# A two-block transformer on one core: feed-forwards that begin with the input matmuls, and conditioning products moved into the context stage

## The chip, the cores and the metric

The kernel runs on one core of one Trainium2 chip. The metric is the device time of one execution in microseconds (us), as the median of several runs. The core has five engines with instruction streams of their own: TensorE (PE: matmuls and, as matmuls with an identity, transposes), VectorE (DVE), ScalarE (ACT), GpSimd (POOL) and SyncE (SP), which here issues the transfers from device memory. Each engine takes its instructions strictly in the order in which the kernel put them.

## The reference, cut to what matters

One sequence of 256 tokens of width 1024 goes through two blocks. The first has two layers; each layer is, with `rmsnorm` around every step:

```
h = h + 0.5 * rmsnorm(swiglu(rmsnorm(h, g[0]), ffn1_w_in[i], ffn1_w_out[i]), g[1])
...  mix = even_mixer (layer 0) or odd_mixer (layer 1)
h = h + rmsnorm(mix, g[3])
h = h + 0.5 * rmsnorm(swiglu(rmsnorm(h, g[4]), ffn2_w_in[i], ffn2_w_out[i]), g[5])
...  a gated per-layer embedding
```

where `swiglu(x, w_in, w_out) = (silu(gate) * up) @ w_out` with a hidden width of 2816. The second block also has two layers, a pooling mixer and an attention, each followed by a squared-relu MLP of hidden width 4096. Its norms are modulated by a conditioning vector, for the main ("latent") tokens and, up to the attention, for 256 context tokens of their own:

```
s_lat, s_ctx = silu(c), silu(c_ctx)
sh1, sc1, g1, sh2, sc2, g2 = split(s_lat @ ada_w[i] + ada_b[i], 6)      # the same with s_ctx for the context
...
h_lat = h_lat + g2 * (square(relu(m_l @ mlp_w1[i])) @ mlp_w2[i])        # layer 0: for the context too
```

`s_lat @ ada_w[i]` needs nothing of the first block, so it can be worked out at any time before it is used.

## The kernel before

All arithmetic is fp32 in effect. A matrix product is three matmuls of split operands (high part by high, high by low, low by high; `mm3`, lines 251 to 254). Weights come as chunks of 128 x 1024 (512 KB) through SP's queue into a ring of four tiles, `rawm`; ScalarE rounds a chunk to its high part `whm` (line 244), VectorE subtracts to get the low part `wlm` in two halves (line 247). Seven such pairs are held; a pair's place comes free when the matmuls of the pair seven chunks earlier are done.

A feed-forward (`ffn`, line 472 on) works through pairs of hidden groups. The first group (`first`) is worked out token-major: matmuls `g` (line 252 to 254, by `group512`), Silu on ScalarE and product with the up part on VectorE (`sil`, line 482), four transposes on TensorE (`tpsm`, line 429), split into `hid`. `rb_of` (line 409) spreads the reciprocal norms over columns (`dg` on VectorE, `rbpm` on TensorE). All later groups (`inp`) are feature-major, without transposes: 48 matmuls `finm` fill a PSUM bank half with gate and half with up, twice per group; VectorE, ScalarE and VectorE again (`sil`, lines 496 to 498) finish it. The output matmuls `acc` follow some groups behind.

The conditioning products are no matmuls: the weights arrive transposed, and VectorE multiplies each 128 x 1024 half chunk (`rawa`) by the conditioning row and sums along it, in one instruction (`ada_chunk`, line 1013, written to a junk tile `jka`; the sum goes to `adacol`). There are 48 chunks of two halves; 32 of them serve latent and context and take two products per half. They are handed out to the feed-forwards and the odd mixer by the list `cuts`, as filling with low priority: a half chunk is loaded by SP between the weight loads. `ada_finish` adds the biases, makes the norm factors and turns the gates into rows in device memory (transposes `adtf`, line 1035).

`mlp0` is the MLP of layer 0 for both token sets. In its loop `both(i)` does 96 matmuls for hidden group i, 24 of the context (`cfinf`) and 24 latent (`mfinm`) by turns; `relu2` takes each PSUM bank through a tile `rl` (ScalarE relu, VectorE square, split into `hich` and `hicl`, or `hidh` and `hidl`); `out(i - 1)` does 24 matmuls `cfof`, which VectorE adds into `ac`, and 24 `acc`. Tiles come from pools; a tile with the same tag as others waits, in the order in which the program asks for them, until an earlier one of its `bufs` buffers is no longer read.

The order within each engine is settled ahead of the run by a scheduler from priorities and from such dependences.

Of the kernel before, what the change touches and what calls it, by code (L numbers as in the profile page):

```python
# [173 lines left out]
def tile_model(ctx: ExitStack, tc: tile.TileContext, A, out):  # L174
# [44 lines left out]
    M = Res()  # L219
# [31 lines left out]
    def mm3(o, a, b, first, last):  # L251
        T.matmul(o, a[0], b[0], start=first, stop=False)  # L252
        T.matmul(o, a[0], b[1], start=False, stop=False)  # L253
        T.matmul(o, a[1], b[0], start=False, stop=last)  # L254

    def hilo(hi, lo, src):
        ins = S.activation(hi, src, AF.Copy)  # L257
# [109 lines left out]
    def junction(acc, gb, mul, e, x, g, pre=None, act=None):  # L367
        def rstd(t):
            sm = ssq2(halves(acc[t]), 1.0 / (32 * mul))
            return ms_r(sm, e[t] if e is not None else epst[:, (0 if mul == 1.0 else 1):(1 if mul == 1.0 else 2)])[1:]  # L370

        def scaled(t, n):
            sl = slice(512 * n, 512 * n + 512)
            y = tp.tile([128, 512], F32, name="yt", tag="yt", bufs=3)
            V.tensor_tensor(y, acc[t][:, sl], gb[:, sl], op=ALU.mult)
            return y

        def add(t, n, y, r):
            sl = slice(512 * n, 512 * n + 512)
            return V.scalar_tensor_tensor(h[:, t, sl], y, r, h[:, t, sl], op0=ALU.mult, op1=ALU.add).ins  # L380

        done_ = [None]

        def step(t):
            with after(done_[0]):
                if pre is not None:
                    pre(t)
                r, _ = rstd(t)
                ys = [scaled(t, n) for n in range(2)]
                for n in range(2):  # L390
                    with after(done_[0]):
                        done_[0] = add(t, n, ys[n], r)
                    if x.xt is not None:
                        ins = feed(x, t, n, g)
            if x.xt is not None and t == 0:
                with tc.issue_after(ins):
                    if act is not None:
                        warm(act)
            if t == 1:
                if x.xt is None:  # L400
                    for t in range(2):
                        stats(x, t)
                elif x.stats:
                    with tc.issue_after(ins):
                        for t in range(2):
                            stats(x, t)
        return step

    def rb_of(x):
        ps = bank(name="rbp")  # L410
# [56 lines left out]
    def feat_tile(ps, w, xt):  # L467
        for k in range(8):
            a = (w[0][:, 128 * k:128 * k + 128], w[1][:, 128 * k:128 * k + 128])
            mm3(ps, a, (xt[0][:, k, :], xt[1][:, k, :]), k == 0, k == 7)  # L470

    def ffn(x, win, wout, np_, pool, hooks, joint, side=None):
        def first():
            hid = xt_tiles(2, pool, "hid", 4)
            ps = group512(win[0:2], x.xt, True)
            for t in range(2):
                if x.r[t] is None:
                    stats(x, t)
            for t in range(2):
                s = pool.tile([128, 256], F32, name="sil", tag="sil", bufs=2)  # L480
                S.activation(s, ps[:, t, 0:256], AF.Silu, scale=x.r[t])
                V.tensor_tensor(s, s, ps[:, t, 256:512], op=ALU.mult)
                t_split(s, 2, hid, t)
            return hid

        hids = [first()]
        rb = rb_of(x)

        def inp(i):
            hid = xt_tiles(2, pool, "hid", 4)  # L490
            for j in range(2):
                ps = bank(name="fin")
                for u in range(2):
                    feat_tile(ps[:, 256 * u:256 * u + 256], split(M, win[2 * i + j], u), x.xt)
                s = pool.tile([128, 256], F32, name="sil", tag="sil", bufs=2)
                V.tensor_tensor(s, ps[:, 0:256], rb, op=ALU.mult)
                S.activation(s, s, AF.Silu)
                V.tensor_tensor(s, s, ps[:, 256:512], op=ALU.mult)  # L498
                hilo(hid[0][:, j, :], hid[1][:, j, :], s)
            return hid  # L500

        acc = None
        for i in range(1, np_):
            hids.append(inp(i))
            if i == 1 and side is not None:
                with behind(seen[0]):
                    side()
            if i == HOLD:
# [123 lines left out]
    def even_block(l, x, nx, ng):  # L632
# [5 lines left out]
        with tc.tile_pool(name="ev", bufs=1, reuse_waits="tile") as ev:  # L638
# [218 lines left out]
            for b in range(2):  # L857
# [5 lines left out]
            out_kn(A["evo"][0], acc, yts[0], 0, True, False)  # L863
            out_kn(A["evo"][2], acc, ys, 0, False, False)
            out_multi([(A["evo"][3], ys, 2), (A["evo"][1], yts[1], 0)], acc, False, True,
                      junction(acc, gb, 1.0, None, x2, ng))
        return x2

    def odd_block(l, x, nx, ng):
# [138 lines left out]
    def ada_chunk(l, i, who, sv, r, jk):  # L1008
        for f in range(2):
            src = r.raw.tile([128, 1024], F32, name="rawa", tag="raw" + r.tag, bufs=2)  # L1010
            Y.dma_start(src, A["adw"][l, i][:, 1024 * f:1024 * f + 1024])
            for v in who:
                V.scalar_tensor_tensor(jk, src, 1.0, sv[v], op0=ALU.mult, op1=ALU.mult,  # L1013
                                       accum_out=adacol[:, l, v, 2 * i + f:2 * i + f + 1])

    def silu_vec(v, tile_):
# [1 line left out]
        S.activation(tile_, tile_, AF.Silu)  # L1018
        return tile_

    def ada_finish(l, v, r, pool):
# [4 lines left out]
        if n == 48:  # L1026
            V.scalar_tensor_tensor(gsc[:, l, v, 1], col[:, 32:40], 1.0, ng2[:, l, 1], op0=ALU.add, op1=ALU.mult)
            stage = pool.tile([128, 2, 8], F32, name="stage", tag="stage", bufs=1)
            if l == 0:
                V.tensor_tensor(stage[:, 0], col[:, 16:24], psc, op=ALU.mult)  # L1030
            else:
                V.tensor_copy(stage[:, 0], col[:, 16:24])
            V.tensor_copy(stage[:, 1], col[:, 40:48])
# [155 lines left out]
    def mlp0(rr, cx, pre):  # L1189
        with tc.tile_pool(name="lm0", bufs=1, reuse_waits="tile") as lm:  # L1190
            g = gload(rows[1])
            gc = cx.rp.tile([128, 1024], F32, name="prow", tag="prow", bufs=3)
            Y.dma_start(gc, rows[3].partition_broadcast(128))
            ac = cx.sp.tile([128, 2, 1024], F32, name="ac")
            xt = xt_tiles()
            al = alloc_in(lm)
# [61 lines left out]
            hids[1][0] = inp((bank(name="mfin"), xt, "hid", w1))  # L1258
            acc = acc_tiles()
            out_l(0, w2, acc, True)  # L1260
            for i in range(2, 16):
                hids.append(both(i))
                if i < 14:
                    out(i - 1, acc)
                if i == 4:
                    for v in range(2):
                        ada_finish(1, v, AD, lm)
            out(13, acc)
            js = (14, 15)
            ws = [split(M, A["m2"][0, j], i) for j in js for i in range(2)]  # L1270
            cxt = xt_tiles(8, cx.xp, "cxT")

            def rstd(t):
                for n in range(2):
# [259 lines left out]
        Y.dma_start(out[128:256, half(0)], hf[:, half(0)])  # L1534
        S.dma_start(out[128:256, half(1)], hf[:, half(1)])

    def side_ada(pool, chunks):
        who = (0, 1) if any(c[2] for c in chunks) else (0,)
        jk = pool.tile([128, 1024], BF16, name="jka1", tag="jka1")
        tiles = [pool.tile([128, 1024], F32, name="sv1", tag="sv1", bufs=2) for _ in who]  # L1540

        def run():
            p = tc.cur_priority
            tc.cur_priority = p + FILL // 2
            r = Res()
            r.raw, r.tag = pool, "s"
            sv = [silu_vec(v, tiles[v]) for v in who]
            for l, i, both in chunks:
                ada_chunk(l, i, (0, 1) if both else (0,), sv, r, jk)
            tc.cur_priority = p  # L1550

        return run
# [6 lines left out]
    AD = Res()  # L1559
    AD.bank, AD.tag = pfl, "f"  # L1560

    def fin0(pool):
        for v in range(2):
            ada_finish(0, v, AD, pool)

    x = new_x()
    for t in range(2):
# [1 line left out]
            feed(x, t, n, gcol[:, 0, 0])  # L1569

    lat = [(0, i, True) for i in range(24)] + [(1, i, i < 8) for i in range(24)]
    cuts = {(0, 1): lat[:9], (0, 2): lat[9:20], (1, 1): lat[20:30], (1, 2): lat[30:45], (1, 0): lat[45:]}

    def plain():
        return new_x(False)
# [6 lines left out]
    for l in range(2):  # L1582
        x = ffn_block(l, 1, x, new_x, gcol[:, l, 1], cuts[l, 1], None if l else {2: setup, 5: rope2})
        x = (odd_block if l else even_block)(l, x, new_x, gcol[:, l, 2])
        x = ffn_block(l, 2, x, plain, None, cuts[l, 2], {5: fin0} if l else None)
        if l == 1:
            cx = Res()
            cx.tag, cx.bank, cx.nsm = "f", pfl, 8
# [57 lines left out]
```

## Time and profile before

| what | value |
| --- | --- |
| runs | 1895.53, 1896.07, 1900.37 us; median 1896.07 |
| profiled execution | 1896.52 us |
| its span, first to last instruction | 1894.5 us |
| busy in the span: PE, DVE, ACT | 97%, 70%, 49% |
| mean granted TensorE clock | 0.992 of full speed |
| HBM read | 349.92 MB, 185 GB/s over the span |

Times in the views count from the start of the span. The idle time of an engine that is not the bottleneck costs nothing. The start of a matmul is exact, its end is modelled, so the pace of a row of matmuls is read from one start to the next.

### The profile page before, as it was taken

The page shows a single profiled execution, that of the slowest core. Times are in us where ns is not written, and L with a number is a line of the kernel's source. Part 1 is how long each engine was busy: PE and PEld are TensorE (multiplying, and loading weights), DVE is VectorE, ACT ScalarE, POOL GpSimd, SP SyncE. Part 2 cuts the span into 40 slices and gives each one's busy share as a digit, 9 for nine tenths or more (in the row PEclk, how much of TensorE's full clock was granted, in tenths as well). Part 3 has the DMA queues.
Part 4 walks back from the last instruction along what each step waited for, and adds up shares of the span by engine and source line. Part 5 has one row for each costly group of instructions (what it writes and reads, how often), then busy time and mean ns, then how long its engine had stood idle before and what let it go on. Part 6 is the DMA issues. An engine that isn't in the chain of part 4 may idle for free.

```text
span 1894.5 us, 29709 instructions
## 1 busy us (share of the span) xinstructions
PE 1834.9 (97%) x11425; PEld 1615.8 (85%) x11425; DVE 1332.2 (70%) x2522; ACT 927.3 (49%) x1463; POOL 57.8 (3%) x96
## 2 busy tenths in 40 slices
PE   7999999999999999999999999899999999999998
PEld 6999777899969998888789898789999987667997
DVE  6998666899679976856588877744444478556555
ACT  6645756644474445444454456533223235544443
POOL 0000000000000000000000000100000002000000
PEclk9999999999999999999999999999999999999999
DMA  7887534788568875755589865432333314226652
GB/s 265 286 284 244 172 101 144 259 274 273 177 215 277 272 241 192 247 172 161 168 282 307 298 195 201 135 110 90 108 96 98 98 60 147 78 68 187 197 191 81
DMA packets 100181, 352.93 MB, mean 186 GB/s; under 512 B 12296, under 2 KB 13128, under 8 KB 100040
## 3 DMA queue, kind: packets, MB, share of 16 engines
q1 hardware_dynamic: 99320, 350.17, 56.7%
q8 instruction: 89, 1.46, 0.3%
q10 hardware_dynamic: 720, 0.88, 0.1%
q14 instruction: 52, 0.43, 0.1%
HBM read 349.92 MB, written 1.08 MB: 185 GB/s over the span
## 4 chain that ended last, share of the span: by engine, by line
PE 85%; DVE 5%; ACT 4%; DMA 3%; issue 2%; POOL 1%; SPq 0%; POOLq 0%; ACTq 0%; DVEq 0%
PE acc L252 8%; PE acc L254 8%; PE acc L253 8%; PE finm L252 7%; PE finm L253 7%; PE finm L254 7%; PE mfinm L253 3%; PE mfinm L252 3%; PE mfinm L254 3%; PE g L254 3%; PE g L252 3%; PE g L253 3%; DMA rawa<-in_adw_dram 2%; PE cfof L252 1%; PE cfof L254 1%
## 5 line engine op out<-in xcount | busy, mean ns | idle before, releaser
L247 DVE TENSOR_TENSOR wlm<-rawm,whm 128x512 fp32r<-128x512 f32 x1048 | 683.5, 686 | 321.3 <-ACT whm L244 318.0
L244 ACT ACTIVATE whm<-rawm 128x1024 fp32r<-128x1024 f32 x524 | 547.6, 1057 | 509.6 <-PE acc L254 133.6
L252 PE MATMUL finm<-xTh,whm 128*128 128x256 f32 x1280 | 359.5, 281 | 3.3 <-DVE sil L498 3.2
L253 PE MATMUL finm<-xTl,whm 128*128 128x256 f32 x1280 | 359.0, 280 | 0.0
L254 PE MATMUL finm<-xTh,wlm 128*128 128x256 f32 x1280 | 359.0, 280 | 0.0
L252 PEld LDWEIGHTS finm<-xTh,whm 128*128 128x128 f32 x1280 | 240.7, 188 | 5.8 <-DVE sil L498 4.3
L254 PEld LDWEIGHTS finm<-xTh,wlm 128*128 128x128 f32 x1280 | 245.1, 192 | 0.0
L253 PEld LDWEIGHTS finm<-xTl,whm 128*128 128x128 f32 x1280 | 240.5, 188 | 1.4
L252 PE MATMUL acc<-whm,hidh 128*128 128x512 f32 x544 | 213.6, 393 | 1.9 <-ACT hidh L257 1.9
L254 PE MATMUL acc<-whm,hidl 128*128 128x512 f32 x544 | 214.3, 394 | 0.0
L1013 DVE SCALAR_TENSOR_TENSOR jka<-rawa,sv 128x1024 bf16<-128x1024 f32 x160 | 195.0, 1219 | 26.3 <-DMA rawa<-in_adw_dram 23.5
L253 PE MATMUL acc<-wlm,hidh 128*128 128x512 f32 x544 | 213.2, 392 | 0.0
L252 PE MATMUL g<-whm,xTh 128*128 128x512 f32 x320 | 130.8, 409 | 9.5 <-DVE xTh L262 3.4
L253 PE MATMUL mfinm<-xTl,whm 128*128 128x256 f32 x480 | 133.0, 277 | 0.0
L252 PE MATMUL mfinm<-xTh,whm 128*128 128x256 f32 x480 | 132.9, 277 | 0.0
L254 PE MATMUL mfinm<-xTh,wlm 128*128 128x256 f32 x480 | 132.9, 277 | 0.0
L254 PE MATMUL g<-whm,xTl 128*128 128x512 f32 x320 | 129.9, 406 | 0.9 <-DVE xTl L349 0.4
L253 PE MATMUL g<-wlm,xTh 128*128 128x512 f32 x320 | 129.7, 405 | 0.0
L252 PEld LDWEIGHTS acc<-whm,hidh 128*128 128x128 f32 x544 | 102.8, 189 | 23.2 <-ACT hidh L257 3.2
L254 PEld LDWEIGHTS acc<-whm,hidl 128*128 128x128 f32 x544 | 102.6, 189 | 21.0 <-DVE hidl L258 0.3
L253 PEld LDWEIGHTS acc<-wlm,hidh 128*128 128x128 f32 x544 | 102.4, 188 | 20.6 <-DVE wlm L247 0.2
L253 PEld LDWEIGHTS mfinm<-xTl,whm 128*128 128x128 f32 x480 | 90.1, 188 | 0.6
(465 smaller groups left out, 3123.9 us busy)
## 6 DMA issues: line engine op xcount, KB each, us to landing
rawm<-in_m_dram SPq DMA_DIRECT2D x128, 512.0 KB, 3.7
rawa<-in_adw_dram SPq DMA_DIRECT2D x96, 512.0 KB, 5.5
rawm<-in_f1i_dram SPq DMA_DIRECT2D x88, 512.0 KB, 5.1
rawm<-in_f2i_dram SPq DMA_DIRECT2D x88, 512.0 KB, 5.2
rawm<-in_odi_dram SPq DMA_DIRECT2D x48, 512.0 KB, 4.2
rawm<-in_f1o_dram SPq DMA_DIRECT2D x40, 512.0 KB, 5.2
rawm<-in_f2o_dram SPq DMA_DIRECT2D x40, 512.0 KB, 5.5
rawm<-in_evi_dram SPq DMA_DIRECT2D x22, 512.0 KB, 4.1
```

The source lines that it names most:

```text
L244: a = S.activation(wh, src, AF.Copy)
L247: v = V.tensor_tensor(wl[:, sl], src[:, sl], wh[:, sl].bitcast(F32), op=ALU.subtract)
L252: T.matmul(o, a[0], b[0], start=first, stop=False)
L253: T.matmul(o, a[0], b[1], start=False, stop=False)
L254: T.matmul(o, a[1], b[0], start=False, stop=last)
L1013: V.scalar_tensor_tensor(jk, src, 1.0, sv[v], op0=ALU.mult, op1=ALU.mult, accum_out=adacol[:, l, v, 2 * i + f:2 * i + f + 1])
```

## The change

1. In every feed-forward the transposes of the first group and `rb_of` (together `turn`) are tied behind the first 48 `finm` matmuls, and take their PSUM bank from another pool; `finm` comes first. `sil` has four buffers instead of two.
2. Statistics of the even mixer's first token half are taken before its second half; its last step loads the Silu table early.
3. `ada_finish` is cut in two: arithmetic (hook 2) and transposes to rows (hook 6).
4. The cuts become 9, 9, 8, 6 chunks for the four feed-forwards and none for the odd mixer (before 9, 11, 10, 15 and 3), and the last 16 chunks, latent only, go into `mlp0` behind `both(2)`. There the half chunks (`rawas`) go into the three buffers of tag `prow`, and the junk tile `jkr` takes tag `rl` with its two buffers.
5. In `mlp0` the gate row `gc` is loaded after the loop.

```
-        hids = [first()]
-        rb = rb_of(x)
+        h0, ss = first()
+        hids, rb = [h0], []
+        F = Res()
+        F.bank, F.tag = pfl, "f"
+
+        def turn(mm):
+            with tc.issue_after(mm):
+                rb.append(rb_of(x, F))
+                for t in range(2):
+                    t_split(ss[t], 2, h0, t, 0, F)
...
         def inp(i):
...
-                    feat_tile(ps[:, 256 * u:256 * u + 256], split(M, win[2 * i + j], u), x.xt)
-                s = pool.tile([128, 256], F32, name="sil", tag="sil", bufs=2)
-                V.tensor_tensor(s, ps[:, 0:256], rb, op=ALU.mult)
+                    mm = feat_tile(ps[:, 256 * u:256 * u + 256], split(M, win[2 * i + j], u), x.xt)
+                if not rb:
+                    turn(mm)
+                s = pool.tile([128, 256], F32, name="sil", tag="sil", bufs=4)
+                V.tensor_tensor(s, ps[:, 0:256], rb[0], op=ALU.mult)
...
-            if i == 1 and side is not None:
+            if i == 2 and side is not None:
...
+                if t == 1 and x.xt is not None and x.stats:
+                    stats(x, 0)
...
-                        for t in range(2):
-                            stats(x, t)
+                        stats(x, 1)
...
-                      junction(acc, gb, 1.0, None, x2, ng))
+                      junction(acc, gb, 1.0, None, x2, ng, act=AF.Silu))
...
     def mlp0(rr, cx, pre):
...
-            gc = cx.rp.tile([128, 1024], F32, name="prow", tag="prow", bufs=3)
-            Y.dma_start(gc, rows[3].partition_broadcast(128))
...
+            side = side_ada(lm, cuts[2, 0], cx.rp)
             for i in range(2, 16):
                 hids.append(both(i))
+                if i == 2:
+                    with behind(seen[0]):
+                        side()
                 if i < 14:
                     out(i - 1, acc)
-                if i == 4:
+                if i == 13:
+                    stages = [ada_finish(1, v, lm) for v in range(2)]
+                if i == 15:
                     for v in range(2):
-                        ada_finish(1, v, AD, lm)
+                        ada_rows(1, v, stages[v], AD, lm)
...
+            gc = cx.rp.tile([128, 1024], F32, name="prow", tag="prow", bufs=3)
+            Y.dma_start(gc, rows[3].partition_broadcast(128))
...
-    def side_ada(pool, chunks):
+    def side_ada(pool, chunks, ring=None):
...
+        def raw():
+            if ring is None:
+                return pool.tile([128, 1024], F32, name="rawas", tag="raws", bufs=2)
+            return ring.tile([128, 1024], F32, name="rawas", tag="prow", bufs=3)
+
+        def junk():
+            return jk if ring is None else pool.tile([128, 1024], BF16, name="jkr", tag="rl", bufs=2)
...
-    cuts = {(0, 1): lat[:9], (0, 2): lat[9:20], (1, 1): lat[20:30], (1, 2): lat[30:45], (1, 0): lat[45:]}
+    cuts = {(0, 1): lat[:9], (0, 2): lat[9:18], (1, 1): lat[18:26], (1, 2): lat[26:32], (1, 0): [], (2, 0): lat[32:]}
...
-        x = ffn_block(l, 2, x, plain, None, cuts[l, 2], {5: fin0} if l else None)
+        x = ffn_block(l, 2, x, plain, None, cuts[l, 2], {2: fin0, 6: fin1} if l else None)
```

How the order of the instructions moves is shown at three places. First TensorE at the start of the first feed-forward, before:

```order
L252 MATMUL g_174<-whm,xTh 128x512
L253 MATMUL g_174<-wlm,xTh 128x512
L254 MATMUL g_174<-whm,xTl 128x512
L429 MATMUL tpsm<-identt,sil 128x128 x2
L252 MATMUL acc<-whm,hidh 128x512
L253 MATMUL acc<-wlm,hidh 128x512
L254 MATMUL acc<-whm,hidl 128x512
L429 MATMUL tpsm<-identt,sil 128x128 x2
L414 MATMUL rbpm<-dg,ones 128x128 x2
L252 MATMUL acc<-whm,hidh 128x512 x2
L253 MATMUL acc<-wlm,hidh 128x512 x2
L252 MATMUL finm<-xTh,whm 128x256
```

And after the change, in two pieces: behind the last `g`, and 48 `finm` later:

```order
L253 MATMUL g_174<-wlm,xTh 128x512
L254 MATMUL g_174<-whm,xTl 128x512
L252 MATMUL finm<-xTh,whm 128x256
L253 MATMUL finm<-xTl,whm 128x256
...
L254 MATMUL finm<-xTh,wlm 128x256
L415 MATMUL rbpf<-dg,ones 128x128 x2
L430 MATMUL tpsf<-identt,sil 128x128 x2
L252 MATMUL finm<-xTh,whm 128x256
L253 MATMUL finm<-xTl,whm 128x256
L430 MATMUL tpsf<-identt,sil 128x128 x2
L254 MATMUL finm<-xTh,wlm 128x256
```

The transposes and `rbpf` have moved from between `g` and the first `finm` to behind the 48th, and the few `acc` matmuls there are gone from this place.

Second VectorE in `mlp0`, before, from the last chunks of `both(3)` on; the steady pattern is halves of `wlm`, the squares `rl`, the low parts `hicl` and `hidl`, and the additions `ac`:

```order
L247 TENSOR_TENSOR wlm<-rawm,whm 128x512 x3
L1070 TENSOR_TENSOR rl<-rl 128x512
L247 TENSOR_TENSOR wlm<-rawm,whm 128x512
L258 TENSOR_TENSOR hidl<-rl,hidh 128x512
L247 TENSOR_TENSOR wlm<-rawm,whm 128x512 x6
L1070 TENSOR_TENSOR rl<-rl 128x512
L258 TENSOR_TENSOR hicl<-rl,hich 128x512
```

After the change, the stretch that holds the last 20 of the 32 products (`jkr`) and the squares of `both(3)`, which are the two `rl` rows:

```order
L247 TENSOR_TENSOR wlm<-rawm,whm 128x512 x4
L1026 SCALAR_TENSOR_TENSOR jkr,adacol<-rawas,sv_12909 128x1024 x3
L247 TENSOR_TENSOR wlm<-rawm,whm 128x512 x2
L1026 SCALAR_TENSOR_TENSOR jkr,adacol<-rawas,sv_12909 128x1024 x2
L247 TENSOR_TENSOR wlm<-rawm,whm 128x512 x2
L1026 SCALAR_TENSOR_TENSOR jkr,adacol<-rawas,sv_12909 128x1024 x13
L1088 TENSOR_TENSOR rl<-rl 128x512
L1037 TENSOR_TENSOR adacol<-adacol,adc 128x48
L1088 TENSOR_TENSOR rl<-rl 128x512
L1038 SCALAR_TENSOR_TENSOR gsc<-adacol,adc 128x8
L258 TENSOR_TENSOR hicl<-rl,hich 128x512
```

The last two `wlm` rows ahead of the 13 products split the first chunk of `both(6)`; the squares of `both(3)` stand behind the 13. On TensorE the rows behind `both(4)` are three `mfinm` matmuls and then the `cfof` of `out(3)`, which read `both(3)`'s `hich`.

Third SP's queue in `mlp0`, before:

```order
L271 DMA gb<-rows 128x1024
L239 DMA rawm<-in_m_dram 128x1024 x18
L1039 DMA rows<-stT 16x128
L239 DMA rawm<-in_m_dram 128x1024 x37
```

And its end after the change, in which `rawas` are the half chunks of the products:

```order
L239 DMA rawm<-in_m_dram 128x1024 x2
L1024 DMA rawas<-in_adw_dram 128x1024 x2
L239 DMA rawm<-in_m_dram 128x1024
L1024 DMA rawas<-in_adw_dram 128x1024 x3
L239 DMA rawm<-in_m_dram 128x1024
L1024 DMA rawas<-in_adw_dram 128x1024 x10
L1295 DMA prow<-rows 128x1024
L239 DMA rawm<-in_m_dram 128x1024 x37
```

Ten half chunks now stand in one row on the queue, ahead of the gate row and the last 37 weight chunks.

## Rows read from the trace of the kernel before

**Rows 1.** The page, section 1: busy us, share of the span, instructions of each engine.
```profile
PE 1834.9 (97%) x11425; PEld 1615.8 (85%) x11425; DVE 1332.2 (70%) x2522; ACT 927.3 (49%) x1463; POOL 57.8 (3%) x96
```

**Rows 2.** Waits of TensorE: us in total, times, longest.
```profile
PE tpsm L429 <- DVE sil L482: 6.2, 4, 2.0
```

**Rows 3.** Timeline of TensorE, third feed-forward's start: start, us, instruction [idle before].
```profile
564.00 0.39 PE L253 MATMUL g<-wlm,xTh 128*128 128x512 f32 x1
564.24 0.39 PE L254 MATMUL g<-whm,xTl 128*128 128x512 f32 x1
566.40 0.44 PE L429 MATMUL tpsm<-identt,sil 128*128 128x128 f32 x2 [1.77 <-DVE sil L482]
...
570.93 0.63 PE L252 MATMUL acc<-whm,hidh 128*128 128x512 f32 x1
571.35 0.38 PE L252 MATMUL finm<-xTh,whm 128*128 128x256 f32 x1
```

**Rows 4.** Timeline of TensorE at the first, second and fourth feed-forward's start.
```profile
23.96 0.39 PE L254 MATMUL g<-whm,xTl 128*128 128x512 f32 x1
...
28.10 0.43 PE L429 MATMUL tpsm<-identt,sil 128*128 128x128 f32 x2
28.37 0.61 PE L414 MATMUL rbpm<-dg,ones 128*128 128x128 f32 x4
28.74 0.77 PE L252 MATMUL acc<-whm,hidh 128*128 128x512 f32 x2
...
29.81 0.28 PE L252 MATMUL finm<-xTh,whm 128*128 128x256 f32 x1
29.93 0.28 PE L253 MATMUL finm<-xTl,whm 128*128 128x256 f32 x1
...
338.92 0.50 PE L254 MATMUL g<-whm,xTl 128*128 128x512 f32 x1 [0.40 <-DVE xTl L349]
...
345.57 0.41 PE L252 MATMUL finm<-xTh,whm 128*128 128x256 f32 x1
...
954.41 0.39 PE L254 MATMUL g<-whm,xTl 128*128 128x512 f32 x1
...
956.05 0.28 PE L1035 MATMUL adtf<-identt,stage 128*16 128x128 f32 x1 [1.14 <-DVE stage L1033]
...
961.82 0.28 PE L252 MATMUL finm<-xTh,whm 128*128 128x256 f32 x1
```

**Rows 5.** Stretches: us, busy of PE, PEld, DVE, ACT, POOL; clock, DMA share, GB/s.
```profile
567.40:571.40 4.00, 4.00 (x14) 3.08 (x15) 3.53 (x8) 3.22 (x5) 0.00 (x0) 0.59 0.67 174
955.00:1130.00 175.00, 169.55 (x1205) 158.45 (x1206) 138.75 (x263) 82.00 (x115) 0.73 (x2) 0.99 0.82 276
1246.00:1290.00 44.00, 44.00 (x292) 39.83 (x291) 20.42 (x33) 12.97 (x16) 0.00 (x0) 1.00 0.31 95
```

**Rows 6.** Waits in 955 to 1130: us in total, times, longest.
```profile
DVE jka L1013 <- DMA rawa<-in_adw_dram: 17.6, 15, 2.3
...
PE finm L252 <- DVE sil L498: 3.2, 3, 1.6
```

**Rows 7.** Prices: the product (page), its transfer (page), a weight transfer in 1246:1290.
```profile
L1013 DVE SCALAR_TENSOR_TENSOR jka<-rawa,sv 128x1024 bf16<-128x1024 f32 x160 | 195.0, 1219 | 26.3 <-DMA rawa<-in_adw_dram 23.5
...
rawa<-in_adw_dram SPq DMA_DIRECT2D x96, 512.0 KB, 5.5
...
rawm<-in_m_dram SPq DMA_DIRECT2D x8, 512.0 KB, 4.0
```

**Rows 8.** Timeline of TensorE in the context stage, first matmul of `out(3)`.
```profile
1289.94 0.39 PE L252 MATMUL cfof<-whm,hich 128*128 128x512 f32 x1
```

**Rows 9.** Timeline of ScalarE and VectorE there.
```profile
1285.68 1.29 DVE L247 TENSOR_TENSOR wlm<-rawm,whm 128x512 fp32r<-128x512 f32 x2 [3.54 <-ACT whm L244]
...
1288.84 0.63 ACT L257 ACTIVATE hich<-rl 128x512 fp32r<-128x512 f32 x1 [0.76 <-DVE rl L1070]
1290.03 1.06 ACT L244 ACTIVATE whm<-rawm 128x1024 fp32r<-128x1024 f32 x1 [0.55 <-PE mfinm L253]
```

More of the change, by code (lines that the diff above doesn't have):

```diff
@@ L253, in mm3 @@
         T.matmul(o, a[0], b[1], start=False, stop=False)
-        T.matmul(o, a[1], b[0], start=False, stop=last)
+        return T.matmul(o, a[1], b[0], start=False, stop=last).ins
     def hilo(hi, lo, src):
@@ L404, in step, with rb_of @@
                     with tc.issue_after(ins):
-                        for t in range(2):
-                            stats(x, t)
-        return step
-    def rb_of(x):
-        ps = bank(name="rbp")
+                        stats(x, 1)
+        return step
+    def rb_of(x, r=None):
+        ps = bank(r, "rbp")
         for t in range(2):
@@ L469, in feat_tile @@
             a = (w[0][:, 128 * k:128 * k + 128], w[1][:, 128 * k:128 * k + 128])
-            mm3(ps, a, (xt[0][:, k, :], xt[1][:, k, :]), k == 0, k == 7)
+            mm = mm3(ps, a, (xt[0][:, k, :], xt[1][:, k, :]), k == 0, k == 7)
+        return mm
     def ffn(x, win, wout, np_, pool, hooks, joint, side=None):
@@ L478, in first @@
                     stats(x, t)
+            ss = []
             for t in range(2):
-                s = pool.tile([128, 256], F32, name="sil", tag="sil", bufs=2)
+                s = pool.tile([128, 256], F32, name="sil", tag="sil", bufs=4)
                 S.activation(s, ps[:, t, 0:256], AF.Silu, scale=x.r[t])
                 V.tensor_tensor(s, s, ps[:, t, 256:512], op=ALU.mult)
-                t_split(s, 2, hid, t)
-            return hid
-        hids = [first()]
-        rb = rb_of(x)
+                ss.append(s)
+            return hid, ss
+        h0, ss = first()
[7 more added lines that the diff above has]
+                    t_split(ss[t], 2, h0, t, 0, F)
         def inp(i):
@@ L493, in inp @@
                 for u in range(2):
-                    feat_tile(ps[:, 256 * u:256 * u + 256], split(M, win[2 * i + j], u), x.xt)
-                s = pool.tile([128, 256], F32, name="sil", tag="sil", bufs=2)
-                V.tensor_tensor(s, ps[:, 0:256], rb, op=ALU.mult)
+                    mm = feat_tile(ps[:, 256 * u:256 * u + 256], split(M, win[2 * i + j], u), x.xt)
+                if not rb:
+                    turn(mm)
+                s = pool.tile([128, 256], F32, name="sil", tag="sil", bufs=4)
+                V.tensor_tensor(s, ps[:, 0:256], rb[0], op=ALU.mult)
                 S.activation(s, s, AF.Silu)
@@ L1006, in ada_consts, with ada_chunk @@
         Y.dma_start(wms.rearrange("p g e c -> p (g e c)"), A["wms"])
-    def ada_chunk(l, i, who, sv, r, jk):
+    def ada_chunk(l, i, who, sv, raw, junk):
         for f in range(2):
-            src = r.raw.tile([128, 1024], F32, name="rawa", tag="raw" + r.tag, bufs=2)
+            src = raw()
             Y.dma_start(src, A["adw"][l, i][:, 1024 * f:1024 * f + 1024])
             for v in who:
-                V.scalar_tensor_tensor(jk, src, 1.0, sv[v], op0=ALU.mult, op1=ALU.mult,
+                V.scalar_tensor_tensor(junk(), src, 1.0, sv[v], op0=ALU.mult, op1=ALU.mult,
                                        accum_out=adacol[:, l, v, 2 * i + f:2 * i + f + 1])
@@ L1019, in silu_vec, with ada_finish @@
         return tile_
-    def ada_finish(l, v, r, pool):
+    def ada_finish(l, v, pool):
         n = 48 if (l == 0 or v == 0) else 16
@@ L1025, in ada_finish, with ada_rows @@
         V.scalar_tensor_tensor(gsc[:, l, v, 0], col[:, 8:16], 1.0, ng2[:, l, 0], op0=ALU.add, op1=ALU.mult)
[L1026 to L1033, printed above, removed]
+        if n < 48:
+            return None
+        V.scalar_tensor_tensor(gsc[:, l, v, 1], col[:, 32:40], 1.0, ng2[:, l, 1], op0=ALU.add, op1=ALU.mult)
+        stage = pool.tile([128, 2, 8], F32, name="stage", tag="stage", bufs=2)
+        if l == 0:
+            V.tensor_tensor(stage[:, 0], col[:, 16:24], psc, op=ALU.mult)
+        else:
+            V.tensor_copy(stage[:, 0], col[:, 16:24])
+        V.tensor_copy(stage[:, 1], col[:, 40:48])
+        return stage
+    def ada_rows(l, v, stage, r, pool):
+        if stage is not None:
             ps = bank(r, "adt")
@@ L1535, in final @@
         S.dma_start(out[128:256, half(1)], hf[:, half(1)])
-    def side_ada(pool, chunks):
+    def side_ada(pool, chunks, ring=None):
         who = (0, 1) if any(c[2] for c in chunks) else (0,)
-        jk = pool.tile([128, 1024], BF16, name="jka1", tag="jka1")
-        tiles = [pool.tile([128, 1024], F32, name="sv1", tag="sv1", bufs=2) for _ in who]
+        if ring is None:
+            jk = pool.tile([128, 1024], BF16, name="jka1", tag="jka1")
+        tiles = [pool.tile([128, 1024], F32, name="sv1", tag="sv1", bufs=len(who)) for _ in who]
+        def raw():
+            if ring is None:
+                return pool.tile([128, 1024], F32, name="rawas", tag="raws", bufs=2)
+            return ring.tile([128, 1024], F32, name="rawas", tag="prow", bufs=3)
+        def junk():
+            return jk if ring is None else pool.tile([128, 1024], BF16, name="jkr", tag="rl", bufs=2)
         def run():
@@ L1544, in run @@
             tc.cur_priority = p + FILL // 2
-            r = Res()
-            r.raw, r.tag = pool, "s"
             sv = [silu_vec(v, tiles[v]) for v in who]
             for l, i, both in chunks:
-                ada_chunk(l, i, (0, 1) if both else (0,), sv, r, jk)
+                ada_chunk(l, i, (0, 1) if both else (0,), sv, raw, junk)
             tc.cur_priority = p
@@ L1560, in tile_model, with fin1 @@
     AD.bank, AD.tag = pfl, "f"
+    stages0 = []
     def fin0(pool):
+        stages0.extend(ada_finish(0, v, pool) for v in range(2))
+    def fin1(pool):
         for v in range(2):
-            ada_finish(0, v, AD, pool)
+            ada_rows(0, v, stages0[v], AD, pool)
     x = new_x()
```

## The prediction

> **What bounds the kernel now.** I first read the page's busy shares [rows 1]: TensorE is busy for 97% of the span, the next engine for 70%. So a microsecond is won where TensorE waits or runs slowly, and it is lost where TensorE is made to wait. Work taken from another engine counts for nothing by itself. I then read TensorE's waits by releaser [rows 2]: the transposes of the first hidden tile wait 6.2 us in all for the four `sil` products on VectorE, once in each feed-forward. The timeline there [rows 3, 4] shows that the wait is not the whole loss. For the conditioning products I read two stretches by engine [rows 5], the waits in the first of them [rows 6], the prices [rows 7] and what stands in the context stage where the products now go [rows 8, 9]. The durations are those of the profiled execution: 1894.5 us span, 1896.5 us in all, 0.4 us above the median of the three runs (1896.07); the sum is made against 1896.5.
>
> **The feed-forward starts (four times).** Before, after the last `g` matmul TensorE waits for Silu and product, does two transposes, waits for the high part, does a few `acc` matmuls among the rest, and only then begins `finm`. A `g` matmul is followed by the next start 0.23 us later [rows 3], so I count from 0.23 us after the start of the last `g` to the first `finm`:
> - third feed-forward: 564.24 + 0.23 to 571.35 = 6.88 [rows 3]
> - first: 23.96 + 0.23 to 29.81 = 5.62; second: 338.92 + 0.23 to 345.57 = 6.42; fourth: 954.41 + 0.23 to 961.82 = 7.18 [rows 4], of which 0.23 is the first of two small conditioning transposes (the second waits 1.14 us for VectorE), so 6.95
>
> What of that is work that stays? In each of the first three stand 7 `acc` matmuls (7 x 0.23 = 1.6), in the fourth 8 (1.8), and the small matmuls: two transposes 28.10 to 28.37 = 0.27, twice, and the row of reciprocals 28.37 to 28.74 = 0.37 [rows 4], 0.91 together, taken as 1.0. The rest is the wait (1.77 in the third) and slow running: `acc` at 570.93 is followed after 0.42 instead of 0.23, and the granted clock of 567.4 to 571.4 is 0.59 [rows 3, 5], a mixture of the levels 1.2 and 2.4 GHz. Now the first 48 `finm` matmuls follow the last `g` at once, and they need only `xT` and weights; their weights stand in the same place of the split order as before, so they are ready. A `finm` starts 0.12 after the one before [rows 4], so these 48 take 5.7 us, and in that time ScalarE and VectorE do their Silu, product and reciprocal, which took 566.40 - 564.47 = 1.9 us to the first transposes. So I take the whole rest as gained: 6.88 - 2.6 = 4.3; 5.62 - 2.6 = 3.0; 6.42 - 2.6 = 3.8; 6.95 - 2.8 = 4.1; together **-15.2 us**. Below that: if VectorE comes late with the turn, the wait alone (6.2) is gained and the slow running partly stays, so -10; above, -16.
>
> **The second feed-forward of block 1 (955 to 1130).** Here the DMA engines are busy 0.82 of the time at 276 GB/s [rows 5], the products on VectorE wait 17.6 us for their columns, and the `finm` matmuls wait 3.2 us, in three places, for VectorE [rows 6]. The change cuts the columns fetched in this stage from 30 transfers to 12 and the products from 34 to 24. VectorE still has 24 products, but its waits for data go, so I take those as gained: **-3.2 us** (0 to -4, the latter with a matmul or two at the lower level behind each). In the other feed-forwards and the odd mixer the products only become fewer where no TensorE wait is put down to them; there it is worth 0, since TensorE's own work covers them.
>
> **The parts that cost nothing.** Statistics of the even mixer's first half ahead of the second, the Silu table at its end, the conditioning finish in two parts (its transposes now stand among `finm` and `acc`, which go on beside the arithmetic), and the gate row loaded later: all lie beside TensorE work of the 5.7 us `finm` blocks or the 11 us groups of the context stage. Without that cover each is a small wait, 1.14 us in the one case that the trace has (`adtf` in the fourth start [rows 4], counted above). I take 0, with +-1.
>
> **The context stage: where it is lost.** In 1246 to 1290 TensorE has no idle time at all, VectorE is busy 20.4 of 44 us, and the DMA engines 0.31 [rows 5]. By these averages 32 products of 1.22 us [rows 7], 39 us, fit into the idle time of several groups. But the products' junk output `jkr` is allotted from tag `rl`, two buffers, which the squared relu's `rl` tiles use too, and in program order all 32 come right after `both(2)`. So `both(3)`'s relu gets its buffers only behind the last two products. VectorE's rows show the result: 13 products in a row, then `rl`. The order before the 13 fixes when they begin: two `wlm` halves of `both(6)`'s first chunk, whose `whm` takes the ring slot that `both(4)`'s second chunk held. In before that `whm` starts at 1290.03 [rows 9], when `both(4)` ends and TensorE begins with `out(3)` at 1289.94 [rows 8]. TensorE's next rows are 3 `mfinm` (0.35 us), then `cfof` of `out(3)`, which needs `both(3)`'s `hich`, so `rl`. TensorE stands from 1290.3.
>
> How long? In before's times: `whm` to 1291.1, two halves 1.29 [rows 9], so the 13 products begin at 1292.4. After the last come the square `rl`, of the same shape as a half (0.65 to 0.7), and the high part `hich` 0.63 [rows 9], with gaps 1.4 together.
> - If their data always lie ready: 13 x 1.22 = 15.9, end 1308.3, `cfof` at 1309.7: stall 19.4.
> - With the ring of three: transfer n+3 is issued only when product n has ended, and takes its landing time L. The first three lie ready; the 13th ends at 1293.6 + 4 x (L + 1.22). With L = 4.0, the median of the same stage's transfers [rows 7], that is 1314.5, and the stall is 1315.9 - 1290.3 = 25.6. With 5.5, the median of the conditioning transfers in the busy feed-forwards [rows 7], it is 31.6.
>
> I take 4.0: during the stall nothing else is loaded, as in the quiet stage, but up to three transfers are under way. Then TensorE restarts at the lower level, as after the shorter wait of the third start: there matmuls stood 0.42 apart until 571.35 [rows 3], which over 567.4 to 571.4 costs 0.41 x 4 = 1.6, say 2. Loss **+27.6 us** (19.4 + 1 to 31.6 + 3).
>
> **Sum.** -15.2 - 3.2 + 27.6 = +9.2: 1896.5 + 9.2 = **1905.7 us**.
>
> **The rivals.**
> 1. The context stage absorbs the products, and only the gains stay: 1896.5 - 18.4 = 1878. For it: VectorE is idle for 54% of that stage and the DMA engines for 69% [rows 5]. Against it: the averages don't count here, since VectorE takes its rows in order and the relu is behind the products. It decides if the relu's rows come ahead of the last products; the order says that they don't. The Trainium skill, "Perfetto Trace Analysis", section Optimization Strategy, says that a kernel with several regimes may gain by interleaving them in addition to tuning each, and this is what would carry the rival: DMA-bound products beside a TensorE-bound stage.
> 2. The stall is only VectorE's own work: the columns land within the time of two further products (2 x 1.22), so that three buffers do. Then 19.4 + 1.6 - 18.4 = +2.6: 1899. For it: the DMA engines are free. Against it: 4.0 is the median of transfers of the same size in this very stage [rows 7].
> 3. The columns land as slowly as in the feed-forwards (5.5): +31.6 + 2 - 18.4 = +15.2: 1911.7. For it: three transfers share the engines. Against: nothing else does.
> 4. The feed-forward starts gain little, because the turn, now among `finm`, is waited for there by `finm` of the next group: VectorE's `rb` product needs the turn's result, and `finm` has few banks. Then the 15.2 shrinks to about 5 and the time is 1916. For it: VectorE and ScalarE are busiest there. Against: the turn has 5.7 us and needs 1.9 plus two short steps.
>
> **How the numbers follow.** Chances: forecast 0.62, rival 1 0.10, rival 2 0.13, rival 3 0.08, rival 4 0.07. The range reaches from rival 2 less a larger start gain (1896) to rivals 3 and 4 (1916), and leaves out rival 1 and the far end of the last. 0.3%, 5.7 us, is about what can be told from no change here: faster means below 1890.4, and slower above 1901.8. Rival 1 gives faster 0.10; rival 2 and the lowest twentieth of the forecast the same, 0.17; the rest is slower, 0.73.
>
> **What would show it.** In the changed kernel's trace: no wait of `tpsm` for `sil` at the starts, and `finm` following `g` without a gap; the `finm` waits for `sil` in the second feed-forward of block 1 gone; one TensorE wait of 19 to 32 us in the context stage on `cfof` for `hich`; 13 products in a row on VectorE ahead of it, from the second group of three on each set waiting for its transfer; and a granted clock near one half right behind. The prediction is wrong if that one wait is missing or short, or if the starts show a new wait of like size.

## The result and the profile after

The changed kernel takes 1920.37 us (median of 4 runs, 1917.16 to 1922.26) against 1896.28 before: a ratio of 1.0124, with a 95% interval of 1.011 to 1.0139. It is slower, as forecast, but by 24 us, not by 9.2, and outside the range (1896 to 1916). The profiled execution took 1918.72 us, its span 1916.9 us, 22.4 more than before.

The page's busy shares (section 1, us and share of the span) answer to [rows 1]:

```profile
PE 1831.3 (96%) x11425; PEld 1613.3 (84%) x11425; DVE 1333.1 (70%) x2522; ACT 923.8 (48%) x1463; POOL 61.5 (3%) x96
```

The work is the same. TensorE's idle time in the span grows by 26 us, from 59.6 to 85.6, while its busy time falls by 3.6. The waits of TensorE (us in total, times, longest) say where:

```profile
PE mfinm L252 <- ACT rl L1087: 32.9, 1, 32.9
...
PE tpsf L430 <- ACT rb L417: 2.1, 1, 2.1
PE cfof L252 <- DVE ac L1251: 1.9, 2, 1.2
```

The wait of `tpsm` for `sil` [rows 2] is gone, and so is that of `finm` for `sil` [rows 6]. One wait of 32.9 us has come, behind `both(4)` in the context stage, where the prediction put it, but three instructions earlier in TensorE's row: it stands on the `mfinm` matmuls that follow `both(4)`, and not on `cfof` for `hich`. They wait for ScalarE's relu (`rl`, line 1087) to empty a PSUM bank, and the relu waits for the shared buffers. ScalarE's rows at the end of the wait show it:

```profile
1309.64 0.60 ACT L1087 ACTIVATE rl<-cfinf 128x512 f32<-128x512 f32 x1 [30.00 <-DVE jkr L1026]
1310.91 0.60 ACT L1087 ACTIVATE rl<-mfinm 128x512 f32<-128x512 f32 x1 [0.67 <-DVE jkr L1026]
```

The timeline of TensorE there, with the third feed-forward's start ahead of it:

```profile
559.15 0.39 PE L254 MATMUL g<-whm,xTl 128*128 128x512 f32 x1
559.38 0.28 PE L252 MATMUL finm<-xTh,whm 128*128 128x256 f32 x1
...
1190.87 0.39 PE L252 MATMUL cfof<-whm,hich 128*128 128x512 f32 x1
...
1278.33 0.28 PE L254 MATMUL mfinm<-xTh,wlm 128*128 128x256 f32 x1
1311.56 0.58 PE L252 MATMUL mfinm<-xTh,whm 128*128 128x256 f32 x1 [32.95 <-ACT rl L1087]
...
1312.37 0.63 PE L252 MATMUL cfof<-whm,hich 128*128 128x512 f32 x1
1312.79 0.63 PE L253 MATMUL cfof<-wlm,hich 128*128 128x512 f32 x1
...
1314.76 0.40 PE L252 MATMUL cfof<-whm,hich 128*128 128x512 f32 x1
1314.99 0.39 PE L253 MATMUL cfof<-wlm,hich 128*128 128x512 f32 x1
```

`finm` follows `g` after 0.23 us, where it took 7.1 before [rows 3]. The first `cfof` of the context stage, at 1190.87, is a landmark: before, it stood at 1206.90.

```profile
1206.90 0.40 PE L252 MATMUL cfof<-whm,hich 128*128 128x512 f32 x1
```

So up to here the changed kernel is 16.0 us ahead. By the `cfof` of `out(3)`, 1312.37 against 1289.94 [rows 8], it is 22.4 behind: 38.5 us are lost between the two. VectorE's timeline in the wait shows how:

```profile
1279.65 1.23 DVE L1026 SCALAR_TENSOR_TENSOR jkr<-rawas,sv 128x1024 bf16<-128x1024 f32 x1 [3.04 <-DMA rawas<-in_adw_dram]
...
1282.45 1.22 DVE L1026 SCALAR_TENSOR_TENSOR jkr<-rawas,sv 128x1024 bf16<-128x1024 f32 x1 [1.57 <-DMA rawas<-in_adw_dram]
...
1283.60 1.29 DVE L247 TENSOR_TENSOR wlm<-rawm,whm 128x512 fp32r<-128x512 f32 x2
1284.96 1.23 DVE L1026 SCALAR_TENSOR_TENSOR jkr<-rawas,sv 128x1024 bf16<-128x1024 f32 x1
...
1292.12 1.22 DVE L1026 SCALAR_TENSOR_TENSOR jkr<-rawas,sv 128x1024 bf16<-128x1024 f32 x1 [1.89 <-DMA rawas<-in_adw_dram]
...
1309.64 1.23 DVE L1026 SCALAR_TENSOR_TENSOR jkr<-rawas,sv 128x1024 bf16<-128x1024 f32 x1
1310.79 0.08 DVE L1026 DVE_READ_ACCUMULATOR jkr<-rawas,sv 128x1 f32 x1
1310.79 0.69 DVE L1088 TENSOR_TENSOR rl<-rl 128x512 f32<-128x512 f32 x1
```

The 13 products run from 1284.96 to 1310.8, 25.8 us or 2.0 each, though each is busy for 1.2: seven of them wait for their transfer, five for 1.3 to 2.3 us, 9.7 us together. The two products in front of the last split wait too, 3.04 and 1.57 us. The stretch of the wait and the one behind it (as [rows 5]: us, busy of the engines, clock, DMA share, GB/s), and the transfers issued in the wait (count, size, median us to landing):

```profile
1278.40:1311.40 33.00, 0.21 (x2) 0.01 (x1) 20.23 (x34) 2.15 (x3) 0.00 (x0) 0.58 0.79 264
1311.00:1316.00 5.00, 4.44 (x15) 3.63 (x16) 5.00 (x13) 4.22 (x7) 0.00 (x0) 0.65 0.03 13
...
rawas<-in_adw_dram SPq DMA_DIRECT2D x12, 512.0 KB, 5.1
```

A landing takes 5.1 us, not 4.0 [rows 7]. With TensorE idle the DMA engines are busy 0.79 of the time. Behind the wait the `cfof` matmuls begin 0.42 us apart at first and 0.23 from 1314.76 on; the granted clock of these 5 us is 0.65, a mixture of the two levels.

### The profile page after: what moved, and what is told of

Same layout as the page of the kernel before. It is cut to its first block, busy times and chain, and to the rows that moved or that the text cites. A ratio compares the mean times of both kernels' runs of the same rounds, so it can differ in the third digit from the quotient of the medians.

```text
span 1916.9 us, 29678 instructions
## 1 busy us (share of the span) xinstructions
PE 1831.3 (96%) x11425; PEld 1613.3 (84%) x11425; DVE 1333.1 (70%) x2522; ACT 923.8 (48%) x1463; POOL 61.5 (3%) x96
## 4 chain that ended last, share of the span: by engine, by line
PE 84%; DVE 5%; DMA 4%; ACT 3%; issue 1%; POOL 1%; SPq 0%; POOLq 0%; ACTq 0%; DVEq 0%
PE acc L254 8%; PE acc L253 8%; PE acc L252 8%; PE finm L252 8%; PE finm L254 8%; PE finm L253 8%; PE g L254 3%; PE g L252 3%; PE g L253 3%; PE mfinm L252 3%; PE mfinm L254 3%; PE mfinm L253 3%; DMA rawas<-in_adw_dram 2%; PE cfof L252 1%; PE cfof L253 1%
## 5 line engine op out<-in xcount | busy, mean ns | idle before, releaser
L252 PE MATMUL mfinm<-xTh,whm 128*128 128x256 f32 x480 | 133.7, 278 | 32.9 <-ACT rl L1087 32.9
L1026 DVE SCALAR_TENSOR_TENSOR jka<-rawas,sv 128x1024 bf16<-128x1024 f32 x128 | 155.7, 1217 | 6.4 <-DMA rawas<-in_adw_dram 5.6
L252 PEld LDWEIGHTS mfinm<-xTh,whm 128*128 128x128 f32 x480 | 90.6, 189 | 33.7 <-ACT rl L1087 33.1
```

Source lines behind the costliest of these rows:

```text
L1026: V.scalar_tensor_tensor(junk(), src, 1.0, sv[v], op0=ALU.mult, op1=ALU.mult, accum_out=adacol[:, l, v, 2 * i + f:2 * i + f + 1])
```

## The experiments

All stand against the kernel before on the same chip; ratios are of that pair, with 95% intervals. Each expectation states its own two theories, A and B.

**Is it the shared buffer?** The junk output is taken away from tag `rl`:

```
-                V.scalar_tensor_tensor(junk(), src, 1.0, sv[v], ...
+                V.scalar_tensor_tensor(junk() or src, src, 1.0, sv[v], ...
...
-            return jk if ring is None else pool.tile([128, 1024], BF16, name="jkr", tag="rl", bufs=2)
+            return jk if ring is None else None
```

> The change, but the products of the context stage write back into their own loaded tile instead of a junk tile of tag rl, so the squared relu's buffers are free of them. Theory A (the relu stands behind all 32 products because of the shared buffers): the 33 us wait is gone, a few small waits of cfof for ac stay (2 to 5 us); 1896.3 - 15.5 + 2 to 5 = 1883 to 1886. Theory B (the load itself, 32 products and 16.8 MB beside the weights, is too much for that stage, whatever the buffers): at least half of the 39 us lost there stays, 1900 or more.

Measured: ratio 0.9976 (0.9967 to 0.9985), 1893.43 us. The 33 us wait is gone; but of the 17 us by which TensorE is ahead at the first `cfof` only 2 to 3 stay in the profiled execution (4.6 by the ratio). TensorE's waits, and VectorE's timeline at the longest of them:

```profile
PE cfof L252 <- DVE ac L1251: 10.0, 3, 4.0
```

```profile
1256.81 1.23 DVE L1026 SCALAR_TENSOR_TENSOR rawas<-rawas,sv 128x1024 f32<-128x1024 f32 x1 [3.19 <-DMA rawas<-in_adw_dram]
...
1258.56 1.22 DVE L1026 SCALAR_TENSOR_TENSOR rawas<-rawas,sv 128x1024 f32<-128x1024 f32 x1
...
1261.52 1.28 DVE L1251 TENSOR_TENSOR ac<-ac,cfof 128x512 f32<-128x512 f32 x2
```

A product waits 3.19 us for its columns, and the `ac` addition that frees `cfof`'s bank comes behind it. So both theories are half right. The shared buffers cost about 25 us of the 39 (by the spans of the two profiled executions; 28 by the ratios). Some 14 us are still lost without them, in the three groups in which the products run; TensorE's waits for `ac` are 10.0 of these, and by the timeline they come from the products' waits in VectorE's row.

**What is each half of the change worth by itself?** The new starts with the old cuts (`cuts` as before, no `side` in `mlp0`):

> The new feed-forward order alone: the cuts of before, no products in the context stage. From the trace of the changed kernel the starts gave 1.1 (first), 4.3, 3.0 and about 4.1 us, 12.5 together; theory A (the order of the start gives it): 1884, with the waits of finm for sil in the second feed-forward of block 1 back (about 3 us). Theory B (much of the 15 us came from fewer products in the feed-forwards): 1889 or more.

Measured: 0.9999 (0.9987 to 1.001), 1896.41 us. Nothing: theory A's 1884 is missed, and the number is on theory B's side. The starts do gain (the last feed-forward's first `g` comes at 930.60 instead of 941.31), and the second feed-forward of block 1 takes it all back. In 940 to 1120 the wait of `finm` for `sil` is now:

```profile
PE finm L252 <- DVE sil L511: 11.1, 5, 4.5
```

And the first `cfof` of the context stage, which was 16 us ahead with the moved products, is where it was before:

```profile
1206.59 0.39 PE L252 MATMUL cfof<-whm,hich 128*128 128x512 f32 x1
```

Then the moved products with the old starts (`first`, `rb_of` and the place of `side` as before):

> The moved products alone: the feed-forward starts as before (transposes first), cuts and context stage as in the change. Theory A (the two parts add up): loss of 39 in the context stage less 3 in the second feed-forward of block 1, 1896.3 + 36 = 1932. Theory B (the stall depends on how early the stage is reached or on the new start's order): below 1925.

Measured: 1.02 (1.0184 to 1.0217), 1935.74 us, near theory A's 1932. The one long wait is 31.4 us here. The old starts cost some 4 us more than in before (`tpsm` waits 10.5 us for `sil` instead of 6.2), so this isn't quite the old start. With the products moved, the new starts are then worth 0.76% or 14 us (a ratio of 1.0124 instead of 1.02), of which some 4 us are the slower old start; with the old cuts they are worth nothing.

**Half the products.** Eight chunks go back to the second feed-forward of block 1:

```
-    ... (1, 2): lat[26:32], (1, 0): [], (2, 0): lat[32:]}
+    ... (1, 2): lat[26:40], (1, 0): [], (2, 0): lat[40:]}
```

> The change with only the last 8 chunks (16 products) in the context stage, the other 8 back in the second feed-forward of block 1. Theory A (the relu of both(3) stands behind the products; a stall comes only if the last product ends after both(4)): 16 products at 2 us from about 1236 end near 1270, before both(4) ends, so no long wait; 2 to 3 us come back in the feed-forward: 1884 to 1888. Theory B (the loss goes with the number of products): half of 39 stays, about 1901.

Measured: 0.9986 (0.9977 to 0.9996), 1895.51 us. No long wait in the context stage, as theory A said: 16 products end before `both(4)` does. But the time is neither theory's (1884 to 1888, or about 1901). The feed-forward with its 28 transfers gives back not 2 to 3 us but about half of the gain (11.1 us ahead of before at its first `g`, 5.3 at the first `cfof` of the context stage), and the context stage 2 more; `finm` waits for `sil` again:

```profile
PE finm L252 <- DVE sil L511: 9.1, 5, 4.9
```

**Transfers or VectorE's work?** In the context stage only the first three half chunks are loaded; the other products read those again:

```
+            if len(held) < 3:
+                held.append(ring.tile([128, 1024], F32, name="rawas", tag="prow", bufs=3))
+                return held[-1], True
+            used.append(0)
+            return held[len(used) % 3], False
```

> The change, but in the context stage only the first three half chunks are loaded; the other 29 products read those again (so the conditioning of layer 1 is worked out from wrong weights). Shared buffers and 32 products stay. Theory A (the products in the row were paced by their transfers, 2 us each, not by VectorE, 1.2 us): more products are done before both(4) ends, 6 stand behind its last split, the wait falls from 33 to about 10 and the small waits for ac by half; 1895 to 1899. Theory B (VectorE's work and the buffers set the wait): 25 or more stays, 1912 or more.

Measured: 0.9985 (0.9975 to 0.9996), 1893.82 us. The long wait is

```profile
PE mfinm L252 <- ACT rl L1088: 10.8, 1, 10.8
```

so of 33 us two thirds go with the transfers, and the buffers with VectorE's own time make the rest, as theory A had it. (The order of the instructions changes with them: 6 products instead of 13 stand behind the last split, so the two thirds hold more than the waits of the 13.) The same for the other place, where the starts' gain was lost: the new starts with the old cuts, and in the second feed-forward of block 1 only two half chunks loaded:

> The new starts alone (cuts of before), but in the second feed-forward of block 1 only the first two of 30 half chunks are loaded; the other products read those again (wrong conditioning weights). Theory A (the starts' gain was lost there because that stage is held by its transfers, 0.89 busy): the waits of finm for sil go from 11 us to under 1 and the gain shows, ratio 0.991 to 0.994, 1881 to 1886. Theory B (the 34 products' time on VectorE, in its fixed order, holds it): ratio 0.997 or more.

Measured: 0.9898 (0.9882 to 0.9913), 1878.85 us. The products, all 34, still stand in VectorE's row, and `finm` waits nowhere. The stretch 960 to 1110 by engine, of before, of the new starts with the old cuts, of those without the transfers, and of the change:

```profile
960.00:1110.00 150.00, 146.72 (x1070) 138.38 (x1069) 124.89 (x233) 69.40 (x92) 0.00 (x0) 1.00 0.86 288
```

```profile
960.00:1110.00 150.00, 138.81 (x967) 130.21 (x966) 118.80 (x222) 64.69 (x87) 0.00 (x0) 0.97 0.84 279
```

```profile
960.00:1110.00 150.00, 150.00 (x1079) 141.59 (x1078) 127.07 (x239) 71.34 (x96) 0.00 (x0) 1.00 0.62 202
```

```profile
960.00:1110.00 150.00, 150.00 (x1079) 141.59 (x1078) 116.13 (x217) 72.15 (x96) 0.00 (x0) 1.00 0.73 242
```

VectorE is as busy in the third as in the first (127 and 125 us), yet TensorE loses nothing: it is the transfers that hold this stage, not the work. Their share of the DMA engines in this stretch is 0.84 to 0.86; the 0.89 of the expectation is not that of the whole stretch. Whether they hold it through the products' columns or through weights that land later was not separated. Nor was it tried what the old starts would gain without these transfers, so this run doesn't say how much of its gain is the starts'.

**Spread out.** One or two chunks are handed to each hidden group from 2 to 12, instead of all to group 2; first with the products writing into their own tile, then with the junk tile in tag `rl` as in the change:

```
-                if i == 2:
-                    with behind(seen[0]):
-                        side()
+                if i < 13:
+                    with behind(seen[0]):
+                        side(i)
...
+            part = chunks if k == 0 else chunks[16 * (k - 2) // 11:16 * (k - 1) // 11]
```

> The change with the 16 chunks of the context stage handed out one or two per hidden group (2 to 4 products of 1.22 us in each 22 us, groups 2 to 12) instead of all at once, and the products written back into their own tile. Theory A (what costs in that stage is that products waiting for transfers stand in VectorE's row ahead of the relu and of the ac additions; spread out, their data lie ready): nearly all of the 15 to 17 us won before that stage stays, time 0.9915 to 0.994 of before, 1880 to 1885. Theory B (each product costs there wherever it stands): loss of 14.6 as in the run with free buffers, ratio 0.9976 again.

> As the run with the chunks spread, but with the junk tile in tag rl as in the change. Theory A (the shared buffers cost only because all 32 products were asked for before the next relu): within 0.3% of the spread run with its own tiles, 1880 to 1887. Theory B (sharing the two buffers costs by itself): a wait of several us in each of 11 groups, 1900 or more.

Measured: 0.9947 (0.9932 to 0.9962), 1887.07 us, with their own tile, and 0.992 (0.9905 to 0.9935), 1882.54 us, with the shared buffers. The first lies just outside the range of its theory A (0.9915 to 0.994), the second inside that of its own (1880 to 1887 us). Both are faster than both kernels, and the shared buffers do no harm when two to four products, not 32, are asked for between two relus. In the second, TensorE has no idle time in the context stage, with DMA at half:

```profile
1205.00:1460.00 255.00, 255.00 (x1659) 232.74 (x1659) 155.57 (x247) 79.83 (x98) 0.00 (x0) 1.00 0.50 159
```

In the first, `cfof` still waits for `ac`:

```profile
PE cfof L252 <- DVE ac L1251: 7.1, 5, 1.6
```

There the order puts two or three products in one row on VectorE, and with the shared buffers the relu parts them. That this is the cause of the 5 us between the two was not tried.

## Why the prediction was wrong, step by step

The mechanism was right: the place (behind `both(4)`), the row of 13 products, the shared buffers (first experiment), the pace set by three buffers and a landing time, the slow restart, and no gap at the starts. The step that failed is the sum's loss term for the context stage: +27.6 in the prediction, 39 measured (4.5 ahead of the stop, 33.9 from the stop to `cfof`, 0.6 behind it). The gains were 2.4 us short besides. By parts, in the profiled execution:

- **The landing time, 4.0 us.** I took the median of a stage in which 8 transfers are issued in 44 us, less than one under way on average; with up to three conditioning transfers under way, and one weight chunk beside them, it is 5.1. By the prediction's own formula, 4 x 1.1 = 4.4 more; measured, the 13 products took 25.8 instead of 22.1 us: +3.7. The rival with 5.5 was nearer. (The first three did not all lie ready either: the third waited 1.54 us.)
- **"The 13 products begin at 1292.4", 2.1 us after TensorE stops.** It was 6.5: 1284.96 against 1278.4. I let the last split follow its `whm` at once, and didn't ask whether the products ahead of it in VectorE's row had their data. They waited 3.04 and 1.57 us. +4.4. The row of `x2` products stood in the excerpt that I quoted.
- **Small waits ahead of the stop, taken as 0.** From the first `cfof` (16.0 us ahead) to the end of `both(4)` (1278.33 against 1289.83, 11.5 ahead) 4.5 us are lost. Some 2.6 of them fall in `out(2)` and `both(4)`, where `cfof` waits for `ac` (1.9 us in all) behind products that wait for transfers. Some 1.5 fall where `mlp0` begins its input matmuls behind a wait of 2.4 us that before has too: over the 4.2 us behind it the granted clock is 0.59 here and 1.00 in before.

```profile
1201.80:1206.00 4.20, 4.15 (x22) 4.15 (x23) 2.18 (x5) 1.88 (x5) 0.00 (x0) 0.59 0.42 125
```

```profile
1217.80:1222.00 4.20, 4.15 (x35) 4.14 (x36) 2.17 (x5) 1.97 (x6) 0.00 (x0) 1.00 0.40 125
```

The products need not be the cause: the run of the starts without transfers has none in this stage and the same 0.59 there. The remaining 0.4 are a slower pace of the matmuls in one group, which is shown with rival 1 below.

- **The restart, 2 us.** About 1: from 1312.37 on the loss grows by 0.6 more, after 0.5 in the first three `mfinm`.
- **The gains, 18.4.** Measured 16.0 at the first `cfof`. Up to the second feed-forward of block 1 the first three starts gave 1.1, 4.3 and 3.0 (first `g` of each stage to the first of the next) for 3.0, 3.8 and 4.3; the fourth and its stage 7.6 for 7.3. The first fell short because the turn waits there: `tpsf` 2.1 us for `rb`, and ScalarE's row shows why.

```profile
31.03 1.06 ACT L244 ACTIVATE whm<-rawm 128x1024 fp32r<-128x1024 f32 x1 [1.46 <-DMA rawm<-in_f1i_dram]
31.99 0.36 ACT L417 ACTIVATE rb<-rbpf 128x256 f32<-128x256 f32 x1
```

`rb` stands behind a `whm` that waits for a weight transfer: again an instruction that waits for data and holds what comes behind it. This is rival 4 in small. Of the 1.3 us that the third start falls short, 1.0 is in the `g` matmuls, which take 14.7 us from the first to the last instead of 13.7; why is open.

Together: -16.0 + 4.5 + 33.9 (1312.37 less the stop at 1278.45) = +22.4 at the first `cfof` of `out(3)`, where the prediction had about +8.

A step beyond size failed as well. **The starts' 15.2 and the stage's 3.2 were added as if independent.** The second experiment shows that the starts by themselves are worth nothing: the next stage was bound by its transfers [rows 5], and TensorE, come 11 us earlier, waited there for them. The row with DMA at 0.82 and the 17.6 us of product waits [rows 6] said so; I used them for a gain of 3.2 and not as a floor of that stage. In the change itself this did no harm, since the 18 transfers had moved.

Rival 1 (the stage absorbs the products) was wrong for this kernel and right for another arrangement: with the products spread over eleven groups and the shared buffers, the stage takes them at a cost of some 4 us (16.5 us ahead of before at its first `cfof`, 12.6 at the first `g` behind it). These 4 us are no waits but a pace. The 96 input matmuls of a group (`cfinf`, `mfinm`), from the first `cfinf` to the next `cfof`, take 11.31 us in all eleven groups; most groups of before take 10.91. First the spread run, then before:

```profile
1262.84 0.28 PE L252 MATMUL cfinf<-cxTh,whm 128*128 128x256 f32 x1
...
1274.15 0.40 PE L252 MATMUL cfof<-whm,hich 128*128 128x512 f32 x1
```

```profile
1257.10 0.28 PE L252 MATMUL cfinf<-cxTh,whm 128*128 128x256 f32 x1
...
1268.01 0.39 PE L252 MATMUL cfof<-whm,hich 128*128 128x512 f32 x1
```

The granted clock is 1.00 in both. The spread run with products in their own tile has the same products and shows this slower pace in one of these groups only, so its cause is open. The Trainium skill, "Perfetto Trace Analysis", section Optimization Strategy, says that performance may be improved by interleaving regimes; the spread run with the shared buffers agrees (ratio 0.992), where the transfers run beside TensorE's work through 255 us without idle time of TensorE. In the change the same products in one block go with a loss of 39 us. Rival 2 did not happen, and rival 4 only in small.

## What to carry to other kernels

An engine's idle share says how much work fits, but not whether it may stand there: in an in-order row an instruction that waits for a transfer holds back everything behind it, so filling work should be handed out in doses that the transfers can keep up with, and its scratch tiles must not share buffers with tiles on the path unless the doses are small. Where transfers hold a stage, as here with the DMA engines busy 0.84 to 0.86, time won ahead of it can be lost in it; look for that floor before adding gains up. Price a landing by how many transfers will be under way, not by the nearest quiet row.

## What the runs showed of the hardware

512 KB landed in 4.0 us (median) in a quiet stage at 95 GB/s, and in 5.1 with up to three conditioning transfers under way, at 264 GB/s and DMA engines busy 0.79. Over the long wait, in which TensorE did nothing, the mean granted clock was 0.58, and it was 0.65 over the 5 us behind it: the matmuls stood 0.42 apart at first and 0.23 from 1314.76 on. The slow restart cost about 1 us, so a wait of 33 us cost no more at its end than the wait of 1.77 us in the third start of before, where the clock was 0.59 over 4 us (1.6 us by the prediction's estimate).

The same wait of 2.4 us at the start of `mlp0` was followed by a granted clock of 0.59 in the change and of 1.00 in before. And matmuls of 256 columns started 0.118 us apart through whole groups or 0.114, both at a granted clock of 1.00.
